# A two-layer mixer network and an attention block on one core: the first block's attention finished in two pairs of heads, the state-space mixer moved in front of it, and w_out's rows reordered

## The chip, the core and the metric

The kernel runs on one core of a Trainium2 chip. Its metric is the device time in microseconds, here the median of three runs. A profiled execution, taken separately, gives the trace; its span goes from the first to the last instruction.

## The reference

Two blocks in a row work on x, 256 tokens by 1024, in float32. The first has two layers, the second one. The change is in the first block, in the mixers of each layer:

```python
xn = rms_norm(h, attn_norm_g[layer])
u_ssm, u_g, v_g, q, k, v = split(xn @ w_in[layer])        # 256, 256, 256, 512, 512, 512 columns
y_ssm  = s5_mixer(u_ssm, ...)        # linear recurrence per 16-channel group, GELU, GLU with w_glu
y_sgu  = spatial_gating(u_g, v_g, ...)   # u * (W_s v + b) over windows of 128
y_diff = diff_attention(q, k, v, ...)    # 4 heads, two soft-maxes each, then rms_norm per head
h = h + concatenate([y_ssm, y_sgu, y_diff]) @ w_out[layer]   # rows 0-255, 256-511, 512-1023
h = h + conv_gated_mlp(rms_norm(h, ffn_norm_g[layer]), ...)
```

The second block (another attention with memory, gates and an output projection) is not touched.

## The kernel before

**Precision and tiling.** A large product is made of three matmuls on parts of the operands: high times high, high times low, low times high. Weights come from HBM as 1 MB pieces (`wraw`) on SyncE's queue, in the order in which `st.add` listed them; ScalarE makes the high part (L152), VectorE the low part (L153), each 128x1024, with five such buffers. Activations are kept transposed, as `xh` and `xl`, in eight blocks of 128 rows by 256 tokens; `mix` holds the mixers' output in that form: blocks 0 and 1 from the state space, 2 and 3 from gating, 4 to 7 from the four heads.

**What sets the order.** The Python code lists the instructions, and a scheduler puts each engine's instructions into one fixed order, by priority and by when its model holds them ready. Priority is the place in the listing, except that the gemms of a layer's mixers stand 3000 places later (`low`), and the weight splits some places later (`SPLIT_...`). Each engine runs its order strictly. The mixers are generators. A plan string says in which order gemms and mixer steps are listed: `k q u A2 S2 v g G* A* S*` for layer 0 means the gemms of k, q and the state-space input u, two steps of the attention, two of the state space, the gemms of v and of the gating inputs, then gating, attention and state space to their ends. Layer 1 has `k u q S6 A2 v g S* G* A* m`, where m is the gemm of the second block's memory values.

**The mixers.** The state space (`ssm_gen`, L885) shuffles its input by 16 small DMAs, transforms it in two halves a=0 and a=1 (L902; VectorE reads each from the bank px), scans along time (L917), forms the states (L920 to L929), and sums in a bank yb the skip taps (`ktap`, L934) and the outputs of the states (`ct`, L941). Then follow GELU (L945), the w_glu product (L951), tanh, add one, the gate product and the split into high and low parts (L962). Gating (`gmlp_gen`, L965) takes its row statistics, then two products in px (L982).
The attention (`diff_gen`, L1090) has eight units, four heads by two query halves q. `scores` makes a score bank, the soft-maxes and their weighted difference; `values`, two units behind, transposes this (bank pt, of which there is one), multiplies by the values, and adds up squares. When all eight are done, one `rsqrt` of 8 columns (nine small VectorE operations, L371 to L381) gives the norm, and for each query half the four heads are scaled, transposed in pt (L1145) and split (L665, L666).

**PSUM.** Four banks `acc` for gemms and for yb, two for scores, one pt, and one px for the small products of the state space and gating.

**w_out** (L1299 to L1306) takes all four `acc` banks, two token halves by two column halves. For each of four pairs of row blocks, in the order `OUT_ORDER`, it issues 24 matmuls, six to a bank: (2, 4, 6, 0) in layer 0, that is gating, heads 0 and 1, heads 2 and 3, state space; (0, 2, 4, 6) in layer 1. The residual sum and the next norm (L1195) follow.

Of the kernel before, what the change touches and what calls it, by code (L numbers as in the profile page):

```python
# [15 lines left out]
AF = mybir.ActivationFunctionType  # L16
# [4 lines left out]
P = 128  # L21
S = 256
# [5 lines left out]
LOW_1 = 3000  # L28
LOW_2 = 29
DMA_STEPS = 3  # L30
PLAN0 = "k q u A2 S2 v g G* A* S*"
PLAN1 = "k u q S6 A2 v g S* G* A* m"
SPLIT_L0 = 200
SPLIT_F0 = 60
# [132 lines left out]
def tile_model(tc, t, out):  # L167
# [26 lines left out]
    def acc():  # L194
        return Bank(nc, pacc.tile([P, 512], F32, name=nm("acc"), tag="acc"))
# [4 lines left out]
    def pst():  # L200
        return Bank(nc, ps.tile([P, 512], F32, name=nm("pt"), tag="t", bufs=PST_BUFS))
# [32 lines left out]


    PLAN = (PLAN0, PLAN1)
    OUT_ORDER = ((2, 4, 6, 0), (0, 2, 4, 6))
    for l in range(LAYERS):
        w = t["w_in"][l]
        if l == 1:  # L240
# [127 lines left out]
    def rsqrt(src, n, scale, dst=None, tag=None):  # L368

        v = sm(n, tag=tag)  # L370
        V.tensor_scalar(v, src, scale, EPS, op0=OP.mult, op1=OP.add)  # L371
        i = sm(n, I32, tag=(tag or "sm") + "i")
        V.tensor_scalar(i, v.bitcast(I32), 1, None, op0=OP.logical_shift_right)
        V.tensor_scalar(i, i, -1.0, float(0x5F3759DF), op0=OP.mult, op1=OP.add)
        y = i.bitcast(F32)
        z = sm(n, tag=tag)
        for it, d in enumerate((8.77e-4, 5.8e-7)):
            V.tensor_tensor(z, y, y, op=OP.mult)
            V.scalar_tensor_tensor(z, z, -0.5 * (1 + d), v, op0=OP.mult, op1=OP.mult)
            o = dst if (it == 1 and dst is not None) else sm(n, tag=tag)  # L380
            V.scalar_tensor_tensor(o, z, 1.5 * (1 + d), y, op0=OP.add, op1=OP.mult)  # L381
            y = o
        return y
# [22 lines left out]
    def tt(o, a, b_, op, eng=None):  # L406
        (eng or V).tensor_tensor(o, a, b_, op=op)  # L407
# [477 lines left out]
    def ssm_gen(l, ut, mix):  # L885
# [36 lines left out]
        for ri in range(2):  # L922
# [4 lines left out]
            p1v, p2v = [x.rearrange("p (j m) -> p j m", j=8)[:, :, :63] for x in (p1, p2)]  # L927
            tt(st_[ri][:, :, 1:], p1v, p2v, OP.subtract if ri else OP.add)
            yield  # L929
        yb = acc()  # L930
        yv = yb.t.rearrange("p (a i m) -> p a i m", a=2, i=4)
        for a in range(2):
            for i in range(4):
# [156 lines left out]
    def diff_gen(l, qts, sc, vv, mix):  # L1090

        ob = [gen(), gen()]
        ss = sm(8)

        def scores(hd, q):
            nk = P * (q + 1)
            bk = pss()
            sv = bk.t.rearrange("p (c k) -> p c k", c=2)[:, :, :nk]
            bk.mm(sv, qts[hd // 2][:, hd % 2, q * P : (q + 1) * P], kz[hd][:, :, :nk])
            bk.mm(sv[:, :, nk - P : nk], identb, maskd.unsqueeze(1).to_broadcast([P, 2, P]), stop=True)  # L1100
            p = gen()
            pv_ = p.rearrange("p (c k) -> p c k", c=2)[:, :, :nk]
            l_ = sm(2)
            softmax_rows(sv, nk, 2, sc[:, q * 8 + hd * 2 : q * 8 + hd * 2 + 2], pv_, l_)
            rl = sm(2)
            V.reciprocal(rl, l_)
            V.tensor_tensor(rl[:, 1:2], rl[:, 1:2], nlam[:, l : l + 1], op=OP.mult)
            V.tensor_scalar(pv_[:, 1, :], pv_[:, 1, :], rl[:, 1:2], None, op0=OP.mult)
            V.scalar_tensor_tensor(pv_[:, 0, :], pv_[:, 0, :], rl[:, 0:1], pv_[:, 1, :], op0=OP.mult, op1=OP.add)
            return p  # L1110

        def values(hd, q, p):
            nk = P * (q + 1)
            bk = pst()
            for kt in range(q + 1):
                T.transpose(bk.t[:, kt * P : (kt + 1) * P], p[:, kt * P : (kt + 1) * P], ident)
            wt_ = gen()
            A.copy(wt_[:, :nk], bk.t[:, :nk])
            po = bk.t[:, S : S + P]
            for kt in range(q + 1):  # L1120
                T.matmul(po, lhsT=wt_[:, kt * P : (kt + 1) * P],
                         rhs=vv[kt][:, hd * P : (hd + 1) * P], start=kt == 0, stop=kt == q)
            A.copy(ob[q][:, hd * P : (hd + 1) * P], po)
            A.activation(p[:, :P], po, AF.Square, accum_out=ss[:, q * 4 + hd : q * 4 + hd + 1])

        units = [(hd, q) for hd in range(4) for q in range(2)]
        ahead = []
        for u in units:
            ahead.append((u, scores(*u)))
            yield  # L1130
            if len(ahead) > 2:
                u, p = ahead.pop(0)
                values(*u, p)
                yield
        for u, p in ahead:
            values(*u, p)
            yield
        rs = rsqrt(ss, 8, 1.0 / P)
        for q in range(2):
            on = ob[q]  # L1140
            ov_ = on.rearrange("p (h e) -> p h e", h=4)
            tt(ov_, ov_, rs[:, q * 4 : q * 4 + 4].unsqueeze(2).to_broadcast([P, 4, P]), OP.mult)
            bk = pst()
            for hd in range(4):
                T.transpose(bk.t[:, hd * P : (hd + 1) * P], on[:, hd * P : (hd + 1) * P], ident)  # L1145
            bv = bk.t.rearrange("p (h s) -> p h s", h=4)
            split_scaled(mix[0][:, 4:8, q * P : (q + 1) * P], mix[1][:, 4:8, q * P : (q + 1) * P], bv, sgl[:, l : l + 1])
            yield


    kmT = const.tile([P, 4, S], F32, name="kmT")
# [670 lines left out]
```

## Time and profile before

| | |
|---|---|
| three runs | 1047.45, 1050.00, 1050.54 us (median 1050.0) |
| profiled execution | 1047.36 us |
| its span | 1045.1 us |
| TensorE (matmul / weight load) | 1001.7 us (96%) / 893.2 us (85%) |
| VectorE, ScalarE, GpSimd | 772.0 (74%), 618.0 (59%), 14.5 us (1%) |
| mean granted TensorE clock | 0.994 |
| layer 0: mixers and w_out | about 40 to 140 us |
| layer 1: mixers and w_out | about 362 to 470 us |

Matmul records overlap, since matmuls are pipelined: one that lasts 0.39 us in its row is followed 0.23 us later by the next. Lengths of stretches are therefore taken from starts.

### The profile page before, as it was taken

Reading aid. Unit: us, or ns where it says so; the run is one execution under the profiler, and the core shown is the slowest. Engines: PE = TensorE matmul, PEld = TensorE weight load, DVE = VectorE, ACT = ScalarE, POOL = GpSimd, SP = SyncE. Lnnn points to the kernel's source line nnn. Section 1 sums busy time; section 2 is a strip of 40 time slices with the busy share of each in tenths; the row PEclk is TensorE's granted clock in tenths of the full one; section 3 lists DMA queues with packets and bytes.
Section 4 is the critical chain, followed back from the end, with each engine's and each line's share of the span. In section 5 each row is a group of like instructions: output and inputs, shape, how many; then the busy total and the mean of one; then the engine's idle time right before and its main releaser. Section 6 shows DMA issues by size and latency. Waiting matters only on the chain.

```text
span 1045.1 us, 18439 instructions
## 1 busy us (share of the span) xinstructions
PE 1001.7 (96%) x7177; PEld 893.2 (85%) x7177; DVE 772.0 (74%) x1561; ACT 618.0 (59%) x1207; POOL 14.5 (1%) x34
## 2 busy tenths in 40 slices
PE   6799899999999999999999999999999999999996
PEld 5677689999998888778999999899787899889995
DVE  6989789887888669758777777776665666446675
ACT  5786567655675577757555555645666555544442
POOL 2000000000000000000000000000000000000000
PEclk9899999999999999999999999999999999999998
DMA  6543153556555544244554655667332535425551
GB/s 193 195 161 129 51 178 125 199 191 208 197 185 168 185 143 162 81 160 157 168 201 163 201 173 190 194 193 239 121 122 81 170 113 182 131 86 195 167 179 40
DMA packets 130494, 166.57 MB, mean 159 GB/s; under 512 B 12050, under 2 KB 103272, under 8 KB 130408
## 3 DMA queue, kind: packets, MB, share of 16 engines
q1 hardware_dynamic: 130376, 165.40, 48.4%
q8 instruction: 56, 0.92, 0.4%
q14 instruction: 30, 0.25, 0.1%
q10 hardware_dynamic: 32, 0.01, 0.0%
HBM read 160.15 MB, written 1.05 MB: 154 GB/s over the span
## 4 chain that ended last, share of the span: by engine, by line
PE 82%; DVE 8%; ACT 6%; issue 2%; DMA 1%; SPq 0%; POOL 0%; ACTq 0%; DVEq 0%; POOLq 0%
PE acc L94 48%; PE ps L94 26%; DVE sgen L407 2%; DVE wlo L153 2%; PE pt L1479 1%; ACT whi L152 1%; ACT sgen L598 1%; ACT gen L1002 1%; DMA wraw<-in_w_in_dram 1%; PE acc L1534 1%; PE acc L1625 1%; DMA wraw<-in_w_mem_kv_dram 1%; PE px L902 0%; DVE sgen L917 0%; PE acc L1536 0%
## 5 line engine op out<-in xcount | busy, mean ns | idle before, releaser
L152 ACT ACTIVATE whi<-wraw 128x1024 fp32r<-128x1024 f32 x294 | 310.0, 1061 | 270.5 <-PE acc L94 145.1
L153 DVE TENSOR_TENSOR wlo<-wraw,whi 128x1024 fp32r<-128x1024 f32 x294 | 358.0, 1222 | 117.1 <-ACT whi L152 115.1
L94 PE MATMUL ps<-xh,whi 128*128 128x256 f32 x736 | 208.9, 285 | 3.2 <-ACT xh L665 3.2
L94 PE MATMUL ps<-xl,whi 128*128 128x256 f32 x736 | 208.5, 283 | 0.2 <-DVE xl L666 0.2
L94 PE MATMUL ps<-xh,wlo 128*128 128x256 f32 x736 | 208.5, 283 | 0.0
L94 PE MATMUL acc<-xh,wlo 128*128 128x256 f32 x544 | 158.1, 291 | 4.3 <-DVE wlo L153 4.3
L94 PE MATMUL acc<-xh,whi 128*128 128x256 f32 x544 | 158.5, 292 | 0.8 <-ACT xh L665 0.7
L94 PE MATMUL acc<-xl,whi 128*128 128x256 f32 x544 | 157.1, 289 | 0.1
L94 PE MATMUL acc<-whi,xh 128*128 128x512 f32 (+1 forms) x416 | 150.6, 365 | 4.7 <-ACT xh L665 3.4
L94 PE MATMUL acc<-wlo,xh 128*128 128x512 f32 (+1 forms) x416 | 151.2, 363 | 1.9 <-DVE wlo L153 1.8
L94 PE MATMUL acc<-whi,xl 128*128 128x512 f32 (+1 forms) x416 | 149.5, 362 | 0.0
L94 PEld LDWEIGHTS ps<-xh,whi 128*128 128x128 f32 x736 | 140.8, 192 | 5.0 <-ACT xh L665 4.1
L94 PEld LDWEIGHTS ps<-xl,whi 128*128 128x128 f32 x736 | 141.1, 192 | 1.5 <-DVE xl L666 0.6
L94 PEld LDWEIGHTS ps<-xh,wlo 128*128 128x128 f32 x736 | 141.1, 192 | 0.0
L94 PEld LDWEIGHTS acc<-xh,wlo 128*128 128x128 f32 x544 | 105.2, 193 | 5.9 <-DVE wlo L153 4.7
L94 PEld LDWEIGHTS acc<-xh,whi 128*128 128x128 f32 x544 | 105.1, 194 | 3.2 <-issue 1.3
L94 PEld LDWEIGHTS acc<-xl,whi 128*128 128x128 f32 x544 | 105.2, 193 | 2.2 <-issue 1.5
L94 PEld LDWEIGHTS acc<-whi,xh 128*128 128x128 f32 x416 | 79.3, 191 | 16.9 <-ACT xh L665 4.8
L94 PEld LDWEIGHTS acc<-wlo,xh 128*128 128x128 f32 x416 | 79.5, 191 | 13.5 <-DVE wlo L153 3.5
L94 PEld LDWEIGHTS acc<-whi,xl 128*128 128x128 f32 x416 | 79.0, 190 | 10.2 <-DVE xl L666 0.3
L94 PE MATMUL acc<-whi,ah 128*128 128x512 f32 x176 | 69.9, 397 | 0.3 <-ACT ah L669 0.3
L94 PE MATMUL acc<-wlo,ah 128*128 128x512 f32 x176 | 69.5, 395 | 0.0
(339 smaller groups left out, 1396.9 us busy)
## 6 DMA issues: line engine op xcount, KB each, us to landing
wraw<-in_w_in_dram SPq DMA_DIRECT2D x58, 1024.0 KB
wraw<-in_w_up_dram SPq DMA_DIRECT2D x44, 1024.0 KB
wraw<-in_w_down_dram SPq DMA_DIRECT2D x22, 1024.0 KB
wraw<-in_w_out_dram SPq DMA_DIRECT2D x12, 1024.0 KB
wraw<-in_w_mem_kv_dram SPq DMA_DIRECT2D x4, 1024.0 KB
gen<-gen SPq DMA_DIRECT2D x48, 64.0 KB
wraw<-in_w_br_b_dram SPq DMA_DIRECT2D x2, 1024.0 KB
wraw<-in_w_br_m_dram SPq DMA_DIRECT2D x2, 1024.0 KB
```

Source lines behind the costliest of these rows:

```text
L94: self.nc.tensor.matmul(out, lhsT=lhsT, rhs=rhs, start=not self.open if start is None else start, stop=stop)
L152: self.nc.scalar.activation(hv, part, AF.Copy)
L153: self.nc.vector.tensor_tensor(lv, part, hv.bitcast(F32), op=OP.subtract)
L407: (eng or V).tensor_tensor(o, a, b_, op=op)
L598: A.copy(pd[ps, hf], bpow[ri][ps, a * 4 : a * 4 + 4])
L1002: A.activation(sq[:, i * 64 : i * 64 + 64], src[:, i * 64 : i * 64 + 64], AF.Square, scale=rstd[:, q : q + 1], accum_out=ss[:, i : i + 1])
L1479: T.transpose(bk.t[:, i * P : (i + 1) * P], p[:, i * P : (i + 1) * P], ident)
L1534: T.matmul(oc, lhsT=pt[:, kt * P : (kt + 1) * P], rhs=vs[0][:, kt, cols], start=kt == 0, stop=False)
L1625: T.matmul(oc, lhsT=pt[:, (i * 2 + kt) * P : (i * 2 + kt + 1) * P], rhs=vb[:, kt, kv * 64 : kv * 64 + 64], start=kt == 0, stop=kt == 1)
```

## The change

Layer 0's plan lists the state space before the attention, and its w_out takes gating, state space, heads 0 and 1, heads 2 and 3. In both layers yb is taken from px in place of `acc`, and the attention normalises, transposes and splits heads 0 and 1 as soon as their four units have their values, and heads 2 and 3 at the end. The sums of squares lie in another order of columns for that.

```diff
-PLAN0 = "k q u A2 S2 v g G* A* S*"
+PLAN0 = "k q u A2 S2 v g G* S* A*"
...
-    OUT_ORDER = ((2, 4, 6, 0), (0, 2, 4, 6))
+    OUT_ORDER = ((2, 0, 4, 6), (0, 2, 4, 6))
...
-        yb = acc()
+        yb = psx()
...
-            A.activation(p[:, :P], po, AF.Square, accum_out=ss[:, q * 4 + hd : q * 4 + hd + 1])
+            A.activation(p[:, :P], po, AF.Square, accum_out=ss[:, hd * 2 + q : hd * 2 + q + 1])
...
+        def finish(hp):
+            rs = rsqrt(ss[:, hp * 4 : hp * 4 + 4], 4, 1.0 / P)
+            bk = pst()
+            bv = bk.t.rearrange("p (h q s) -> p h q s", h=2, q=2)
+            for q in range(2):
+                on = ob[q][:, hp * S : (hp + 1) * S]
+                ov_ = on.rearrange("p (h e) -> p h e", h=2)
+                tt(ov_, ov_, rs.rearrange("p (h q) -> p q h", q=2)[:, q].unsqueeze(2).to_broadcast([P, 2, P]), OP.mult)
+                for h in range(2):
+                    T.transpose(bv[:, h, q], on[:, h * P : (h + 1) * P], ident)
+            k = 4 + hp * 2
+            split_scaled(mix[0][:, k : k + 2, :].rearrange("p h s -> p (h s)"),
+                         mix[1][:, k : k + 2, :].rearrange("p h s -> p (h s)"), bk.t, sgl[:, l : l + 1])
+
+        done = []
+        def take_values():
+            (hd, q), p = ahead.pop(0)
+            values(hd, q, p)
+            done.append(hd)
+            yield
+            if len(done) % 4 == 0:
+                finish(hd // 2)
+                yield
+
         for u in units:
             ahead.append((u, scores(*u)))
             yield
             if len(ahead) > 2:
-                u, p = ahead.pop(0)
-                values(*u, p)
-                yield
-        for u, p in ahead:
-            values(*u, p)
-            yield
-        rs = rsqrt(ss, 8, 1.0 / P)
-        for q in range(2):
-            on = ob[q]
-            ov_ = on.rearrange("p (h e) -> p h e", h=4)
-            tt(ov_, ov_, rs[:, q * 4 : q * 4 + 4].unsqueeze(2).to_broadcast([P, 4, P]), OP.mult)
-            bk = pst()
-            for hd in range(4):
-                T.transpose(bk.t[:, hd * P : (hd + 1) * P], on[:, hd * P : (hd + 1) * P], ident)
-            bv = bk.t.rearrange("p (h s) -> p h s", h=4)
-            split_scaled(mix[0][:, 4:8, q * P : (q + 1) * P], mix[1][:, 4:8, q * P : (q + 1) * P], bv, sgl[:, l : l + 1])
-            yield
+                yield from take_values()
+        while ahead:
+            yield from take_values()
```

## Rows read from the trace of the kernel before

**Rows 1.** The page's first part: engine, busy us (share of the span), instructions.
```profile
PE 1001.7 (96%) x7177; PEld 893.2 (85%) x7177; DVE 772.0 (74%) x1561; ACT 618.0 (59%) x1207; POOL 14.5 (1%) x34
```
**Rows 2.** Windows of both layers' mixers: length, busy per engine, clock, DMA.
```profile
90.00:106.00 16.00, 13.49 (x83) 10.23 (x82) 13.86 (x50) 10.86 (x43) 0.00 (x0) 1.00 0.36 131
106.00:120.00 14.00, 10.51 (x169) 7.31 (x168) 12.69 (x41) 5.53 (x20) 0.00 (x0) 1.00 0.04 9
...
420.00:450.00 30.00, 30.00 (x164) 23.33 (x162) 21.03 (x60) 21.30 (x68) 2.14 (x4) 1.00 0.20 70
```
**Rows 3.** Chain of waits, end of w_out in layer 0: start, us, what.
```profile
119.76 1.20 PE acc L94 x4
...
123.82 15.38 PE acc L94 x68
```
**Rows 4.** Timeline, the state space behind its second transform, VectorE and ScalarE.
```profile
106.27 0.69 DVE L407 TENSOR_TENSOR sgen<-px,tab 128x512 f32<-128x512 f32 x1 [0.72 <-PE px L902]
106.88 0.68 DVE L670 TENSOR_TENSOR xl<-sgen,xh 128x512 fp32r<-128x512 f32 x1
...
115.31 0.17 DVE L373 TENSOR_SCALAR sm<-sm 128x8 int32<-128x8 int32 x1
...
115.43 0.68 DVE L407 TENSOR_TENSOR sgen<-sgen,sgen 128x504 f32<-128x504 f32 x1
...
119.75 1.28 ACT L945 ACT_TABLE_LOAD   x1
...
121.04 0.60 ACT L945 ACTIVATE sgen<-acc 128x512 f32<-128x512 f32 x1
...
123.85 0.84 ACT L955 ACTIVATE sgen<-px,bgh 128x256 f32<-128x256 f32 x2 [1.64 <-PE px L951]
...
125.53 0.63 ACT L957 ACTIVATE sgen<-sgen 128x512 f32<-128x512 f32 x1
...
126.81 1.30 DVE L407 TENSOR_TENSOR sgen<-sgen,sgen 128x512 f32<-128x512 f32 x1
...
128.15 0.64 ACT L665 ACTIVATE xh<-sgen 128x512 fp32r<-128x512 f32 x1 [1.04 <-DVE sgen L407]
```
**Rows 5.** Timeline of TensorE: skip taps, second transform, first and last w_out matmul.
```profile
83.57 1.37 PE L94 MATMUL acc<-ut,ktap 128*128 128x256 f32 x8
...
104.04 1.07 PE L902 MATMUL px<-sgen,bt 128*128 128x64 f32 x8
...
106.54 0.50 PE L94 MATMUL acc<-whi,xh 128*128 128x512 f32 x1
...
139.53 0.39 PE L94 MATMUL acc<-whi,xl 128*128 128x512 f32 x1
```
**Rows 6.** Timeline of ScalarE: gating's statistics, last exponential, last sum of squares.
```profile
91.21 1.06 ACT L152 ACTIVATE whi<-wraw 128x1024 fp32r<-128x1024 f32 x1 [1.00 <-PE acc L94]
92.17 0.40 ACT L971 ACTIVATE sgen<-vt 128x256 f32<-128x256 f32 x1
...
106.91 0.57 ACT L1087 ACTIVATE gen<-ps,sm,sc 128x256 f32<-128x256 f32 x1
...
114.38 0.20 ACT L1124 ACTIVATION_READ_ACCUMULATOR gen<-pt 128x1 f32 x1
```
**Rows 7.** Timeline of layer 1: output products, w_glu product, table load for exponentials.
```profile
413.14 2.00 PE L94 MATMUL acc<-sgen,ct 128*32 128x64 f32 x128
...
418.75 2.00 PE L951 MATMUL px<-sgen,wglu 128*128 128x256 f32 x8 [0.63 <-ACT sgen L945]
...
423.37 1.28 ACT L1087 ACT_TABLE_LOAD   x1
```
**Rows 8.** Timeline of VectorE in layer 1: first step of the attention's reciprocal root.
```profile
447.55 0.17 DVE L371 TENSOR_SCALAR sm<-sm 128x8 f32<-128x8 f32 x1 [3.37 <-ACT gen L1124]
```
**Rows 9.** Timeline of TensorE, and its window, after a long idle time.
```profile
44.52 0.58 PE L94 MATMUL acc<-xh,wlo 128*128 128x256 f32 x1 [4.01 <-DVE wlo L153]
...
44.50:49.60 5.10, 5.08 (x24) 5.08 (x25) 5.10 (x11) 4.11 (x17) 0.99 (x2) 0.50 0.00 2
```

## The prediction

> **What bounds the kernel now.** I read the busy line first: TensorE holds 1001.7 of 1045.1 us [rows 1], so a change can win only out of the 43 us in which it stands still, unless it alters the work, and it doesn't: the matmuls and transposes are the same in number. Then the windows around the first layer's mixers [rows 2]: from 90 to 106 us TensorE lacks 2.5 us, from 106 to 120 3.5, and after that nothing up to 140. Those 6.0 us are all there is to win in layer 0. VectorE is the fuller engine there (12.7 of 14 us between 106 and 120). In layer 1's mixers, 420 to 450 us, TensorE is full (30.00 of 30), because the memory-value product lies under them.
>
> The chain of waits and the timeline show the order. w_out has 96 matmuls, four groups of 24, one group for two row blocks. Group 2 (gating) starts at 106.54 [rows 5], 18 of its 24 run before the attention is done; group 4 waits for the attention to 119.76; from 123.82 on 68 matmuls take 15.38 us without a break, 0.226 each [rows 3], and the last starts at 139.53 [rows 5]. The state-space rows (hi part from 128.15 on [rows 4]) are last in line and hold nobody up.
>
> **What the change does to that.** Matmuls into one bank keep program order: each w_out bank takes its rows as OUT_ORDER has them. With (2, 0, 4, 6) the state-space group is second, so the attention groups wait behind it in all four banks. After the change the end of w_out is set by R, the time at which the state-space rows are ready: three groups, 72 x 0.226 = 16.3 us, follow R. Today's end is 139.53 + 0.23 = 139.8, so the change breaks even at R = 139.8 - 16.3 = 123.5. Today's R is 128.15 + 0.64 = 128.8. The question is whether the state-space chain gains 5.3 us.
>
> **Its chain, step by step.**
> - *Input transform of half a=1.* It needs the one px bank, which the gating mixer uses from its second product until shortly before 104; it starts at 104.04 [rows 5], VectorE at 106.27 [rows 4]. Gating stays ahead of the state space in the plan, so this start stays, except for what gating itself gains (below).
> - *VectorE.* From 106.27 to 116.1 the chain occupies 9.8 us; nine other operations lie in it, the first the gating low part at 106.88, the last a reciprocal-root step at 115.31 [rows 4], by their start times 2.0 us together (0.6 gating, 1.4 attention). Its own share is 7.8. In front of the attention only gating's 0.6 must come first: 114.7. Where a chain operation waits for the one before, attention steps will still slip in. Bounds: none and all of the attention's 1.4 plus the first pair's finish, about 2.1 (nine small steps at 0.1, which is what the one at 115.31 holds the next operation up, two half-width products at 0.35, a low part at 0.6). I take 0.5, nearer to none because most junctions have a second chain operation ready: 115.2.
> - *Output products.* 128 short matmuls, 2.00 us in layer 1 where nothing breaks them [rows 7]. In layer 0 they are broken at present by the attention's transposes and end at 119.7. Now 117.2.
> - *GELU.* Table load 1.28 plus 0.60 [rows 4]: 119.1.
> - *w_glu product* 2.00 [rows 7]: 121.1. *Tanh pair* 0.84: 121.95. *Add one* 0.63: 122.6. *Gate product* 1.30: 123.9. *High part* 0.64: 124.55 [rows 4]. At present two weight splits push themselves between the last steps; the banks' waiting time lets these be made earlier, since group 2 frees its weight buffers near 112. If they still stand there, R is 1.5 later: 0.84 between the tanh's end at 124.69 and the add, 0.65 between its end at 126.16 and the product [rows 4].
>
> So R = 124.55 without any lead. **The lead:** the skip-tap matmuls (ktap) fill an accumulator now up to 84.94, on a full TensorE; the last eight of the sixteen take 1.37 us [rows 5], all of them so 2.7. In px they can run only after the a=1 transform is read, near 108; there they lie under VectorE's stretch. What is queued behind them at 82, the last gating product, ends up to 2.7 us sooner. Gating's own statistics stand on ScalarE at 92.17 right behind a weight split that waited 1.00 us for TensorE [rows 6]. Bounds 0 and 2.7; I take 0.7, under the 1.00 of that wait, which is the nearest row: the rest of gating's chain waits for VectorE, which doesn't become freer. R = 123.85, and the end 140.2: 0.4 later than now.
>
> **The rest of the edits.**
> - *yb in px.* It frees an accumulator: the six group-2 matmuls that now wait for its release after the GELU (121.64) run before 113, in an idle stretch; already in the sum. px is held through the GELU; nobody else asks for it then, because gating comes before in layer 0 and after the w_glu product in layer 1.
> - *Finishing in pairs.* Per layer nine more small VectorE steps (0.17 each alone, 447.55 [rows 8], about 0.2 apart); the normalising products are four of half width for two of full width. In layer 1 VectorE has gaps (21.0 of 30 us) and TensorE is full, so nothing. New is a wait: the first pair's finish takes the one pt bank between the fourth and fifth value units; queued behind it on TensorE and ScalarE are those four units' transposes and copies. That is 1.6 to 3 us of root steps, 0.7 product, 0.6 transposes, 0.7 and 0.75 splits: about 5 us. The attention's last sum of squares is read at 114.58 [rows 6] and its first rows come at 119.7; five later is some 123 to 125 with the second finish. Group 6 needs them at R + 48 x 0.226 = 134.7, so 10 us of cover. Without that cover this would cost its whole 5.
> - *The swapped plan* issues no DMA in another place, as the shuffle copies belong to the steps before; the order of w_out's loads changes, and that costs nothing: the chain waits for none of them between 119.76 and 139 [rows 3]. The last exponential is over at 107.5 [rows 6] and the GELU comes after it, so no second table switch in layer 0.
> - *Layer 1* keeps its order and is full on TensorE [rows 2]: 0, with bounds of -0.7 and +0.7 for gaps at its seams. Behind it all other code is the same; a shifted list of instructions may win or lose 1 us there.
>
> A rule on table switches would say more. ScalarE pays 1.28 us for the load here and the GELU starts 1.29 us after the load does [rows 4]; in layer 1 the switch back is 1.28 too, and no idle time stands in front of it [rows 7]. The Trainium skill (ScalarE: Activation LUTs, What ACT_TABLE_LOAD costs) counts a drain with every switch, 2.66 us in all. By that R would be 1.4 us later and the end 141.6. The trace shows no such drain in front of a load, so I stay with 1.28.
>
> **Sum.** +0.4 in layer 0, about 0 elsewhere: 1047.36 of the profiled execution becomes 1047.8. Its three timed runs reached 1047.45 to 1050.54, mean 1049.3; on that scale 1049.5, half a microsecond under the median shown. 0.3% (3.15 us) is about what can be told from no change.
>
> **Rivals.**
> 1. *Faster: the chain leads and gaps fill.* If the a=1 transform slips in front of gating's use of px, or gating gains the whole 2.7, R falls to 119 to 122. TensorE then sets the end: of the 6.0 us idle some 2.5 remain: -3.5, so 1046. For it: gating's statistics start only at 92.17 [rows 6], and its products need px after that. Against: px was as free before and was not taken early. With small gains elsewhere it reaches -5. Chance 0.3.
> 2. *Slower: the swap doesn't speed the chain.* If attention steps and weight splits keep their places, R stays between 126.7 and 128.8, while w_out now stands behind it: 128.8 + 16.3 = 145.1, +5.3, so 1054.5. It decides from R = 126.65 on (+3.15). For it: VectorE is 91% full there, and the far bounds together (1.4 + 2.1 - 0.5 on VectorE, 1.5 by weight splits) add 4.5 to R. Against: priority alone should move most of them. Chance 0.17.
> 3. *Slower: the clock.* Between group 2 and R TensorE has only scraps. At 44.5 us, after TensorE had stood still for 4.01, the clock granted was 0.50 for 5.1 us, its lower level of 1.2 GHz [rows 9]: some 2.5 us lost. With +0.4 and a late R: +3.5, 1053. Against: from 106 to 120 TensorE is 75% busy and keeps 1.00 [rows 2], and the skip taps and values now fall into that time. The Trainium skill (TensorE: Matmul & The Clock Gate, HAM oscillation) warns of idle gaps between bursts; the trace's stretch from 44.5 us agrees. Chance 0.08.
>
> **How the numbers follow.** No measurable change 0.45, own range 1047 to 1052; rival 1 0.3; rivals 2 and 3 0.25. From these: faster 0.3, same 0.45, slower 0.25. The range reaches into both: 1044.5 (rival 1 with -5) to 1054.5 (rival 2).
>
> **What would show it.** Right: group 2 complete near 112; then no w_out matmul until R near 124; after it one unbroken run of 72 and the residual's transposes near 140; the skip taps after 107. Each step's mark: VectorE's last state near 115.2, the GELU's end near 119, the first attention pair's split near 110, its second by 125. Wrong: w_out matmuls of the attention before the state-space rows (then order in the bank isn't what I think), R under 120 or over 126.6, a granted clock under 1.00 between 112 and 126, or an exponential with its own table load behind the GELU.

## The result, and the profile after

The changed kernel is slower. Its median over five runs is 1056.62 us (1053.95 to 1058.19), that of the kernel before on the same chip 1049.35; the ratio is 1.0067 with an interval of [1.0046, 1.0088], 7.0 us. The forecast was 1049.5 with a range up to 1054.5. The profiled execution of the changed kernel took 1053.95 us, its span is 1052.2.

The first part of its page (engine, busy us, share of the span, instructions) answers to [rows 1]: the matmuls are the same 7177, VectorE has 22 instructions more, ScalarE two.

```profile
PE 1007.0 (96%) x7177; PEld 894.4 (85%) x7177; DVE 774.7 (74%) x1583; ACT 620.0 (59%) x1209; POOL 14.3 (1%) x34
```

Two executions don't begin their mixers at the same moment, so I count from a mark M, the start of the ten transform matmuls of half a=0, which no edit touches. The two rows of before, from TensorE's timeline (start, us, engine, line, what), are M and the first transposes of the residual behind w_out's last matmul:

```profile
87.70 1.23 PE L902 MATMUL px<-sgen,bt 128*128 128x64 f32 x10
...
139.77 0.60 PE L1208 MATMUL pt<-ident,xraw 128*128 128x128 f32 x4
```

The same timeline of the changed kernel, with the steps of layer 0 that matter:

```profile
86.28 1.22 PE L902 MATMUL px<-sgen,bt 128*128 128x64 f32 x10
...
101.91 1.90 PE L902 MATMUL px<-sgen,bt 128*128 128x64 f32 x16
...
112.84 1.88 PE L94 MATMUL px<-sgen,ct 128*32 128x64 f32 x120
114.92 0.77 PE L1138 MATMUL pt<-ident,gen 128*128 128x128 f32 x4 [0.19 <-DVE gen L407]
...
117.87 3.01 PE L951 MATMUL px<-sgen,wglu 128*128 128x256 f32 x8 [1.95 <-ACT sgen L945]
120.67 0.42 PE L1116 MATMUL pt<-ident,gen 128*128 128x128 f32 x1
...
124.45 0.80 PE L94 MATMUL acc<-whi,xh 128*128 128x512 f32 x1 [0.38 <-ACT xh L665]
125.04 0.63 PE L94 MATMUL acc<-wlo,xh 128*128 128x512 f32 x1
...
137.40 0.68 PE L1138 MATMUL pt<-ident,gen 128*128 128x128 f32 x4 [0.19 <-DVE gen L407]
...
145.65 0.60 PE L1220 MATMUL pt<-ident,xraw 128*128 128x128 f32 x4
```

From M to the residual it was 139.77 - 87.70 = 52.07 us; it is 145.65 - 86.28 = 59.37. That is +7.3, about the whole loss: the spans differ by 7.1 us, since M came 1.4 us earlier (in both executions the clock was at half rate ahead of M, for 6.8 us before and 3.4 here) and the stretch to layer 1's w_out took 1.2 us more. The state-space rows are ready at 124.45, 38.17 behind M. But the attention's fifth unit is transposed only at 120.67 (L1116) and the second pair at 137.40; before, the last sum of squares of the last unit was read at 114.58 [rows 6].

ScalarE's timeline of the changed kernel shows what came between:

```profile
102.27 0.28 ACT L1124 ACTIVATE gen<-pt 128x128 f32<-128x128 f32 x1
...
115.36 0.46 ACT L1087 ACTIVATE gen<-ps,sm,sc 128x128 f32<-128x128 f32 x1 [3.45 <-DVE tab L407]
...
115.93 1.28 ACT L945 ACT_TABLE_LOAD   x1
117.22 0.60 ACT L945 ACTIVATE sgen<-px 128x512 f32<-128x512 f32 x1
...
118.41 1.28 ACT L1087 ACT_TABLE_LOAD   x1
119.71 0.46 ACT L1087 ACTIVATE gen<-ps,sm,sc 128x128 f32<-128x128 f32 x1
...
123.22 0.57 ACT L1087 ACTIVATE gen<-ps,sm,sc 128x256 f32<-128x256 f32 x1
...
138.12 0.69 ACT L665 ACTIVATE xh<-pt,sgl 128x512 fp32r<-128x512 f32 x1 [3.00 <-PE pt L1138]
```

Exponentials (L1087) stand ahead of the GELU at 117.22 and behind it, with a table load of their own at 118.41. The last exponential of before was at 106.91 [rows 6].

VectorE's timeline of the changed kernel, the first step and the last of each pair's reciprocal root:

```profile
102.68 0.17 DVE L371 TENSOR_SCALAR sm<-sm 128x4 f32<-128x4 f32 x1 [0.30 <-ACT gen L1124]
...
114.04 0.15 DVE L381 SCALAR_TENSOR_TENSOR sm<-sm,sm 128x4 f32<-128x4 f32 x1
114.11 0.42 DVE L1080 TENSOR_REDUCE sm<-ps 128x2 f32<-128x256 f32 x1
...
133.01 0.17 DVE L371 TENSOR_SCALAR sm<-sm 128x4 f32<-128x4 f32 x1 [4.38 <-ACT gen L1124]
...
136.63 0.16 DVE L381 SCALAR_TENSOR_TENSOR sm<-sm,sm 128x4 f32<-128x4 f32 x1
```

Nine steps that take 1.8 us when nothing comes between (the second pair's in e2 below) took 11.5 for the first pair, since the state space goes first on VectorE. On TensorE the finish's transposes (114.92) stand ahead of the fifth unit's (120.67) in the one bank pt, so units 5 to 8 wait for the finish. The row maxima of the seventh unit (L1080) come right behind the last step, at 114.11.

Windows of the changed kernel (length, busy us of TensorE, its weight loads, VectorE, ScalarE, GpSimd, then the granted clock, the DMA engines' busy share and GB/s):

```profile
90.00:106.00 16.00, 11.18 (x58) 7.71 (x58) 13.58 (x53) 8.61 (x32) 0.00 (x0) 1.00 0.28 96
106.00:120.00 14.00, 11.45 (x171) 9.05 (x172) 10.38 (x31) 6.27 (x9) 0.00 (x0) 0.95 0.23 77
...
116.00:118.00 2.00, 0.13 (x1) 0.13 (x2) 0.00 (x0) 1.99 (x3) 0.00 (x0) 1.00 1.04 362
118.00:120.00 2.00, 2.00 (x7) 1.66 (x8) 0.75 (x1) 1.97 (x3) 0.00 (x0) 0.67 0.09 32
120.00:122.00 2.00, 1.13 (x5) 0.43 (x3) 1.50 (x6) 1.34 (x6) 0.00 (x0) 0.50 0.02 5
...
128.00:130.00 2.00, 2.00 (x10) 1.53 (x9) 0.56 (x3) 1.02 (x3) 0.00 (x0) 0.77 0.00 0
```

Against [rows 2] TensorE is busy 0.9 us more between 106 and 120, where the skip taps now lie, and 2.3 less between 90 and 106. After 116 to 118, busy for 0.13 of 2 us, its clock was at the lower level, 1.2 GHz, from about 118.7 to 128.9: w_glu's product took 3.01 us where 2.00 was reckoned, and w_out's first products follow each other 0.43 us apart and not 0.23.

### The profile page after: what moved, and what is told of

Its sections match the earlier page's. It is cut to its first block, busy times and chain, and to the rows that moved or that the text cites. A ratio compares the mean times of both kernels' runs of the same rounds, so it can differ in the third digit from the quotient of the medians.

```text
span 1052.2 us, 18463 instructions
## 1 busy us (share of the span) xinstructions
PE 1007.0 (96%) x7177; PEld 894.4 (85%) x7177; DVE 774.7 (74%) x1583; ACT 620.0 (59%) x1209; POOL 14.3 (1%) x34
## 4 chain that ended last, share of the span: by engine, by line
PE 84%; DVE 7%; ACT 5%; issue 2%; DMA 2%; SPq 1%; POOL 0%; ACTq 0%; POOLq 0%; DVEq 0%
PE acc L94 48%; PE ps L94 27%; DVE wlo L153 2%; DVE sgen L407 2%; PE pt L1491 1%; ACT whi L152 1%; DMA wraw<-in_w_in_dram 1%; PE pt L1121 1%; ACT gen L1002 1%; PE acc L1546 1%; PE px L902 1%; PE px L94 1%; PE acc L1637 1%; ACT sgen L598 1%; DMA gen<-in_lambda_k_dram 1%
## 5 line engine op out<-in xcount | busy, mean ns | idle before, releaser
L153 DVE TENSOR_TENSOR wlo<-wraw,whi 128x1024 fp32r<-128x1024 f32 x294 | 358.2, 1222 | 118.2 <-ACT whi L152 116.1
```

The lines of the kernel that those rows point to most:

```text
L153: self.nc.vector.tensor_tensor(lv, part, hv.bitcast(F32), op=OP.subtract)
```

## The experiments

Twelve kernels ran. Columns of times: ratio to the kernel before in the same job, median, and from the one profiled execution of each the distance from M to w_out's end in layer 0; in that stretch, how long TensorE stood idle and how long its clock was at half rate (granted clock 0.50, 1.2 GHz); the distance from there to w_out's end in layer 1; and the part of it that is layer 1's own (its gemms, mixers and w_out). The other part, ahead of it, is layer 0's MLP, which no edit touches.

| kernel | ratio [95% interval] | median us | M to end, layer 0 | idle in it | half rate in it | layer 1 | its own part |
|---|---|---|---|---|---|---|---|
| before | 1 | 1049.35 | 52.07 | 6.0 | 0 | 330.53 | 116.7 |
| changed | 1.0067 [1.0046, 1.0088] | 1056.62 | 59.37 | 9.4 | 10.2 | 331.71 | 117.0 |
| e2 pairs only | 1.0038 [1.0022, 1.0054] | 1053.03 | 53.50 | 6.2 | 0 | 333.64 | 117.5 |
| e4 bank only | 0.9978 [0.9965, 0.9990] | 1047.03 | 52.40 | 5.8 | 3.4 | 329.34 | 116.0 |
| e5 swap only | 1.0035 [1.0019, 1.0051] | 1053.33 | 56.87 | 8.9 | 3.4 | 331.25 | 116.7 |
| e6 changed, no pairs | 1.0013 [1.0000, 1.0026] | 1050.56 | 55.17 | 7.9 | 3.4 | 329.52 | 116.2 |
| e7 changed, no swap | 1.0005 [0.9995, 1.0015] | 1050.04 | 52.01 | 5.5 | 0 | 332.16 | 117.0 |
| e1 changed, finishes late | 1.0035 [1.0019, 1.0050] | 1052.28 | 56.68 | 7.3 | 10.2 | 330.46 | 115.9 |
| e8 first finish after six units | 1.0039 [1.0027, 1.0051] | 1053.40 | 58.74 | 7.8 | 13.7 | 330.02 | 116.7 |
| e9 e1 with the old rows | 1.0029 [1.0017, 1.0041] | 1052.00 | 58.95 | 9.2 | 10.2 | 329.48 | 116.1 |
| e3 own small tiles | 1.0061 [1.0041, 1.0082] | 1055.41 | 59.31 | 10.9 | 6.8 | 330.58 | 115.8 |
| e11 finishes late in layer 1 | 1.0058 [1.0043, 1.0072] | 1056.19 | 59.28 | 10.3 | 6.8 | 330.89 | 115.9 |
| e10 extra products | 1.0101 [1.0085, 1.0116] | 1061.02 | 63.02 | 9.7 | 6.8 | 330.92 | 116.6 |
| e12 bank in layer 1 only | 0.9980 [0.9969, 0.9991] | 1047.89 | 54.54 | 5.7 | 6.8 | 329.78 | 115.9 |

**The clock in these figures.** TensorE is busy for 46.1 us between M and w_out's end before and for 49.9 in the changed kernel, though the matmuls are nearly the same (358 and 354 records). So +7.3 is 3.4 us more of idle time and 3.9 of longer work, since for 10.2 us it ran at half rate. Windows of that stretch (columns as above), before, changed, e1, e6:

```profile
87.70:139.77 52.07, 46.06 (x358) 36.16 (x357) 42.54 (x131) 29.55 (x86) 0.00 (x0) 1.00 0.40 128
86.28:145.65 59.37, 49.93 (x354) 38.27 (x353) 44.41 (x144) 31.54 (x87) 0.00 (x0) 0.91 0.35 113
87.67:144.35 56.68, 49.35 (x355) 38.34 (x354) 43.43 (x144) 30.44 (x86) 0.00 (x0) 0.91 0.38 122
86.80:141.97 55.17, 47.23 (x355) 37.19 (x354) 42.51 (x133) 30.29 (x86) 0.00 (x0) 0.97 0.37 119
```

The timed runs say about the same. Each has its mean granted clock on record, and with it the time at half rate: 18 us on average over the 81 runs of the kernel before, 28 in the changed kernel, 28 in e1, 25 to 27 in e3, e10 and e11, 23 in e5 and e8, 22 in e9, 20 in e6 and e7, 16 to 17 in e2, e4 and e12. Between runs of one kernel, 1 us more at half rate goes with 0.30 us more of time (a fit over these 81 runs and the 107 of the other kernels, each kernel on each chip about its own mean; it takes up 81% of the scatter). By this estimate about 3 of the changed kernel's 7.0 us, and about 3 of e1's 3.7, go with the lower clock. Differences of one profile by a microsecond or two, and those between kernels with unlike clocks, are to be read with that in mind.

The theory after the comparison of traces was that the first pair's finish holds up units 5 to 8 (finish theory). Its rivals: the new order of work does it whatever the finish does (order theory), and TensorE's clock does it.

**e1: both finishes after the eighth unit**

```diff
             done.append(hd)
             yield
-            if len(done) % 4 == 0:
-                finish(hd // 2)
-                yield
...
         while ahead:
             yield from take_values()
+        for hp in range(2):
+            finish(hp)
+            yield
```

> The changed kernel with one thing undone: both pairs of heads are finished after the eighth value unit, none in the middle. Holding theory (the first pair's finish, listed between the fourth and fifth value units, keeps the later units waiting, because the small tiles and the bank pt are handed out in listing order while its root steps wait behind the state space on VectorE): all exponentials come before the GELU, no extra table loads (1 at the GELU, none behind), the state-space rows are ready 2 to 3 us sooner, TensorE's clock stays at 1.00 between 112 and 130, and the time falls by 5 to 8 us against the changed kernel, to 1048 to 1052 (0.998 to 1.002 of before). Order theory (the loss is w_out standing behind the state-space rows, whatever the attention does): nothing of this, 1054 to 1058.

About half of the loss is gone, 1052.28 against the 1048 to 1052 that the holding theory allowed. The exponentials are ahead of the GELU, and one table load stands there. The clock stayed at 1.00 from 112 to 130 as expected, but in this profile it stood at half rate from 93.9 to 104.1 us, the a=1 transform came 18.84 behind M in place of 15.63, and the state-space rows were 1.0 us later and not earlier. TensorE's idle time is 7.3 us against 9.4, only 1.3 above before. So what is left of the loss goes with the clock for the most part, and not with the order of work alone.

**e2: the pairs alone, in the kernel before** (plan, row order and yb's bank as before)

```diff
+        def finish(hp):
...
-        rs = rsqrt(ss, 8, 1.0 / P)
...
+            if len(done) % 4 == 0:
+                finish(hd // 2)
+                yield
```

> The kernel before with only the finishing in two pairs (old plan, old order of w_out, yb in an accumulator). Holding theory: in front of the state space the first pair's root steps have priority on VectorE, so they take 2 to 3 us and not 11; the last exponentials move by about 5 us but stay before the GELU; w_out gets heads 0 and 1 early, near 110. Time 1046 to 1051, no clock loss. If instead the finish in the middle is bad in any plan: 1053 or more. Order theory: nothing is lost without the new order, 1047 to 1051.

The pairs cost 4.0 us with the attention first, too: the answer "bad in any plan", and the holding theory missed. The first pair's root steps took 6.2 us (103.31 to 109.53) where 2 to 3 were expected. In this profile layer 0 gives 1.4 of the cost and the stretch to layer 1's end 3.1, but only 0.8 of that lies in layer 1's own part; the rest lies in layer 0's MLP, where the clock was at half rate for 3.4 us from 147.0 on.

**e3: the changed kernel, the finish's root steps in small tiles of their own**

```diff
-    SM_BUFS = {"sme": 2, "sth": 2, "smi": 3, "smg": 6, "smgi": 2}
+    SM_BUFS = {"sme": 2, "sth": 2, "smi": 3, "smg": 6, "smgi": 2, "smf": 8, "smfi": 2}
...
-            rs = rsqrt(ss[:, hp * 4 : hp * 4 + 4], 4, 1.0 / P)
+            rs = rsqrt(ss[:, hp * 4 : hp * 4 + 4], 4, 1.0 / P, tag="smf")
```

> The changed kernel, the pair's root steps with small tiles of their own (8 and 2 buffers), so that the soft-max of the units behind it isn't in line behind them; the bank pt is still held. Holding theory, by small tiles alone: exponentials of unit 7 at about 103 in place of 115, and the one of unit 8 with them, most of the loss comes back: 1048 to 1052. By tiles and pt together: unit 7 early, unit 8 still behind the GELU with one or two extra table loads, a part comes back: 1051 to 1055. If neither matters: as the changed kernel, 1054 to 1058.

No gain that can be told. Unit 7's exponentials moved ahead of the GELU, unit 8's stayed behind it: the pattern of the second answer without its gain. The small tiles held unit 7, but they alone don't make the loss; the bank pt stays a candidate. A second bank for the finish would show it alone, but all eight are taken, so it wasn't tried.

**e4: yb in px alone, in the kernel before**

```diff
-        yb = acc()
+        yb = psx()
```

> The kernel before with only yb in px instead of an accumulator. Rival theory (px, of which there is one, held through skip taps, output products and GELU, is what costs): 1053 or more. Holding and order theories: the skip taps move from 82 into idle time near 108 and the fourth w_out bank starts earlier, 1046 to 1050, the gating part of w_out 0.7 us or so sooner.

The one edit that pays, by 2.3 us; the interval ends under 1. TensorE is busy 13.49 of the 14 us from 106 to 120, against 10.51 before [rows 2], and 2.2 us less from 90 to 106, so in layer 0 the idle time is only moved (5.8 us against 6.0). In all ten kernels with the bank in layer 0 TensorE now stands still for 2.97 us from 4.05 behind M, where it was busy before.

**e5: the swap alone, in the kernel before**

```diff
-PLAN0 = "k q u A2 S2 v g G* A* S*"
+PLAN0 = "k q u A2 S2 v g G* S* A*"
...
-    OUT_ORDER = ((2, 4, 6, 0), (0, 2, 4, 6))
+    OUT_ORDER = ((2, 0, 4, 6), (0, 2, 4, 6))
```

> The kernel before with the state-space mixer put ahead of the attention and w_out's rows in the new order, and nothing else: no pairs, the output products still in an accumulator. The finish theory (the pairs hold up units 7 and 8, and the new order only exposes it): all exponentials of the first layer stand ahead of the GELU, two table loads fewer than in the changed kernel, w_out ends within 2 us of before, 1048 to 1051 us. The order theory (putting the state space first leaves the attention's last steps between w_out's products whatever the finish does): 1052 us or more, as with the finishes put late (1052.3). The clock theory: half rate between 106 and 130 in either case, and then 1053 or more.

It costs 3.7 us by itself, and all exponentials are ahead of the GELU, so the order theory holds for this part: 2.9 us more of idle time. The clock theory's signs came too (half rate from 115.0 to 118.4, over 1053), and a part of the 3.7 goes with it. TensorE's timeline of this kernel: the state-space rows come at 125.53, 37.71 behind M, and the attention's two finishes now lie between w_out's products.

```profile
125.53 0.50 PE L94 MATMUL acc<-whi,xh 128*128 128x512 f32 x1 [1.73 <-ACT xh L665]
...
131.65 0.63 PE L1145 MATMUL pt<-ident,gen 128*128 128x128 f32 x4
...
134.08 0.60 PE L1145 MATMUL pt<-ident,gen 128*128 128x128 f32 x4
```

**e7: the changed kernel without the swap**, that is the diff of e5 backwards

> The changed kernel with the old plan and the old row order, so pairs and the output products off the accumulators. If the parts add up: pairs alone 1.0038 and the bank alone 0.9978 give 1.0016, 1051 us, and then the swap is worth the remaining 5 us of the changed kernel. If the pairs' cost comes from the waits for VectorE behind the state space, and those are there in either order: 1050 to 1052 with w_out's end 1 to 2 us later than with the bank alone. If the loss is the bank's together with the pairs (both now ask for banks that other steps use): 1055 as in the changed kernel.

1050.04: bank and pairs add up within the scatter (1051 by adding), and layer 0 is as short as before. The swap on top makes 1.0067 of 1.0005, 6.5 us, against 3.7 by itself (e5). So swap and pairs seem to make each other worse by some 2.8 us: with the attention first the pairs cost 2.8 (e4 to e7), behind the state space twice that (e6, below). The intervals of the four kernels leave this as 0 to 6 us, and the changed kernel has, with e1, the lowest clock.

**e8: the first finish after the sixth unit's values**

```diff
-            if len(done) % 4 == 0:
-                finish(hd // 2)
+            if len(done) in (6, 8):
+                finish(len(done) // 2 - 3)
```

> The changed kernel with the first pair's finish written after the sixth unit's values instead of the fourth, so behind the eighth unit's scores; everything else as changed. The finish theory (the steps of units 7 and 8 are handed their tiles behind the finish's): both units' exponentials come before the GELU, one table load fewer in the stage, the first pair's transposes still ahead of the second's, 1051 to 1053 us, no worse than with both finishes last (1052.3). A rival, that any finish ahead of the last values costs what it cost in the change: 1055 or more. The clock theory alone does not tell it from the finish theory.

1.0039 against the changed kernel's 1.0067 (the intervals overlap from 1.0046 to 1.0051), and no worse than e1: the place of the first finish is worth about 3 us. Both units' exponentials came before the GELU, with one table load, as the finish theory has it. What is left does not go away with it; this profile has 13.7 us at half rate and 1.8 us more of idle time than before.

**e9: e1 with w_out's rows in the old order**

```diff
-    OUT_ORDER = ((2, 0, 4, 6), (0, 2, 4, 6))
+    OUT_ORDER = ((2, 4, 6, 0), (0, 2, 4, 6))
```

> The changed kernel with both finishes after the eighth unit, as in the run with the finishes put late, and besides w_out's rows in the order of before (state-space rows last). If what is left of the loss there (1052.3) is that the state-space rows stand early in w_out: 1049 to 1051. If the attention's rows are now the late ones (their last transposes at 130.6 us there, the state-space rows at about 123), then the 24 products of the state-space rows no longer fill the wait and come behind it, 24 x 0.226 us = 5.4 us at most: 1054 to 1057.

Neither: 1052.0 against 1052.28 in e1. Which group of rows stands second makes no difference in time that can be told here, while state space and attention both end late. In the two profiles e9 has 1.9 us more of idle time; by the timed runs' clocks e1 stood longer at half rate.

**e10: nine products more, to keep TensorE busy at 116 us**

```diff
         A.activation(yg, yb.t, AF.Gelu_apprx_tanh)
+        if l == 0:
+            wb = psx()
+            s3 = st_[1].rearrange("p j m -> p (j m)")
+            for _ in range(9):
+                T.matmul(wb.t[:, :S], lhsT=ident, rhs=s3[:, :S], start=True, stop=True)
```

> The changed kernel with nine products of the identity by the last state tile added in the first layer, behind the output products and ahead of w_glu's, into a bank that nobody reads: about 9 x 0.24 us = 2.1 us of TensorE work in the gap from 115.9 to 117.9 us. Nothing else is changed. The clock theory: the stretch from 118.5 to 128.5 keeps its full rate, w_glu's product takes 2.0 us instead of 3.0 and the products behind it 0.23 instead of 0.43 us apart, and the kernel gains 1.5 to 3 us: 1053.5 to 1055. If the half rate is only a companion of the loss (what waits there is the attention, not TensorE): full rate, and the time stays within 1 us of 1056.6. If the gap is not what lowers the clock: half rate and the same time.

Inconclusive, and my mistake: there is one bank px, so the products waited for the GELU to read yb and then stood ahead of w_glu's product. In the trace they are 18 matmuls and not nine, and took 5.84 us and not 2.1. TensorE's timeline of this kernel:

```profile
118.75 5.84 PE L950 MATMUL px<-sgen,ident 128*128 128x256 f32 x18 [1.96 <-ACT sgen L945]
...
124.65 1.99 PE L956 MATMUL px<-sgen,wglu 128*128 128x256 f32 x8
```

The state-space rows came 4.8 us later behind M than in the changed kernel and w_out's end 3.65 later, so w_out's end still follows those rows.

**e11: both finishes late in layer 1 only**

```diff
-            if len(done) % 4 == 0:
+            if l == 0 and len(done) % 4 == 0:
                 finish(hd // 2)
...
+        if l == 1:
+            for hp in range(2):
+                finish(hp)
+                yield
```

> The changed kernel with both finishes after the eighth unit in the second layer only; the first layer as changed. From one w_out's end to the next the changed kernel took 331.71 us in its profile, the one with the finishes late in both layers 330.46 and the one before 330.53. If the pairs cost something in the second layer too, as these rows say: 1.2 us less than the change, 1055.4, and that distance back at 330.5. If that distance only scatters from run to run: 1056.6 within 0.7.

The times don't decide: 1056.19 agrees with the second answer, the ratio of 1.0058 (1055.4 beside the changed kernel's own before) with the first. Layer 1's own part does: 115.9 us here, in e1 and (116.1) in e9, which all have the bank and late finishes there; 117.0, 116.6 and 117.0 in the changed kernel, e10 and e7, which have the bank and the early finish. So the early finish costs about 1 us there. In e3, where it has small tiles of its own, the part took 115.8 us, as without it.

**e12: yb in px in layer 1 only, in the kernel before**

```diff
-        yb = acc()
+        yb = psx() if l else acc()
```

> The kernel before with the output products off the accumulators in the second layer only. With the bank in both layers the second layer took 1.2 us less from w_out's end to w_out's end (329.34 against 330.53 in the profiles) and w_glu's product there came 4.0 us earlier, while the first layer saw a half-rate stretch from 95 to 98.5 us that the kernel before does not have. If the gain is the second layer's and the first gives none: 1047.6, with full rate from 90 to 106. If the first layer's share counts (1047.0 with both): 1048 or more. If the whole of it is scatter: 1049.

0.9980, the same as with the bank in both layers: the gain is layer 1's as far as the times tell, though one profile's stretch there shows only 0.75 us of the 2.1 (1.2 in e4), nearly all in layer 1's own part (115.9 against 116.7). About 1 us more goes with the clock, by the estimate above: 16 us at half rate against 20 in the kernel before of the same job. This kernel and e4 beat both the kernel before and the changed one; between them there is nothing to tell.

**e6: the changed kernel without the pairs** (one finish for all heads after the eighth unit, as before)

```diff
-        yb = acc()
+        yb = psx()
...
-PLAN0 = "k q u A2 S2 v g G* A* S*"
+PLAN0 = "k q u A2 S2 v g G* S* A*"
...
-    OUT_ORDER = ((2, 4, 6, 0), (0, 2, 4, 6))
+    OUT_ORDER = ((2, 0, 4, 6), (0, 2, 4, 6))
```

> The changed kernel with the attention heads finished as before, after all eight units, by token halves and not by pairs of heads; the new plan, row order and bank stay. If the parts add up (swap alone 1.0035, bank alone 0.9978): 1.0013, 1050.9 us; what the kernel with both finishes late has above that (1.0035) is then the pairs themselves, in the second layer most of all, where w_out's end to w_out's end took 333.6 us with pairs alone against 330.5 before. If the swap leaves the bank nothing to give: 1.0035 as with the finishes late, 1053.

1.0013, what adding gives. So the changed kernel's +7.0 us is, with the pairs taken last: bank -2.3, swap +3.7, pairs 1.0067 - 1.0013 = 0.0054 or +5.7. Of these 5.7 the pairs cost 2.3 when both finishes come late (e1 over e6), and the early place of the first the other 3.4. The 2.3 is hardly the finish's own: e1's profile has less idle time than e6's (7.3 us against 7.9), and its timed runs stood 7 us longer at half rate, some 2.1 us by the estimate. The 3.4 is at an equal clock (28 us in both): 2.1 us of idle time in layer 0 and about 1 in layer 1.

## Why the prediction was wrong

**What held.** In e6, where the attention finishes as before, the state-space chain is the one that the prediction worked out, and TensorE's timeline shows its result:

```profile
86.80 1.23 PE L902 MATMUL px<-sgen,bt 128*128 128x64 f32 x10
...
117.32 1.99 PE L951 MATMUL px<-sgen,wglu 128*128 128x256 f32 x8 [0.86 <-ACT sgen L945]
...
122.78 0.50 PE L94 MATMUL acc<-whi,xh 128*128 128x512 f32 x1
```

Predicted was R = 123.85 on before's clock, 36.15 behind M; it is 122.78 - 86.80 = 35.98. In the changed kernel, too, the steps came as said up to the output products: the a=1 transform at 101.91, 15.63 behind M, where 16.34 less a lead of 0.7 was forecast. That a table load has no drain in front of it held in its new place: at 118.41 it begins 0.01 us behind the end of the instruction ahead of it.

**What failed, by steps.**

1. *"About 5 us" of wait for pt, with "10 us of cover" for the attention's rows.* This is the step that broke. The forecast gave the state space the front place on VectorE for its own chain, but did not carry through that the finish's nine root steps then stand behind that same chain: 11.5 us and not 1.6 to 3. With pt next in line for it, units 5 to 8 waited for it. The second pair's transposes were forecast by 125, 37.3 behind M; they came 51.1 behind it. Moving only that finish behind unit 6 brought 0.28% (e8), putting it late 0.32% (e1), taking the pairs out 0.54% (e6). And even without pairs (e6) the last transposes came 43.2 behind M, 10 later than before (33.1): the forecast's 37.3 for them was kept in no version of the swap. That the bank pt is what holds units 5 to 8 is read from TensorE's order and left over by e3; no run frees it alone.

2. *"The last exponential is over at 107.5 and the GELU comes after it, so no second table switch."* 107.5 was read from an execution in which the attention goes first. In the changed kernel units 7 and 8 get their maxima at 114.11 and 120.37, so the GELU stands between exponentials, and a second load of 1.28 us with it. Together with w_glu's product at half clock (3.01 for 2.00), R came at 38.17 behind M, 2.0 later than forecast.

3. *"72 x 0.226 = 16.3 us follow R."* The product count was right, the stretch was not: it took 145.65 - 124.45 = 21.2 us in the changed kernel and 141.97 - 122.78 = 19.2 in e6, where pairs play no part. Between the 72 products lie the attention's transposes and value products, which the forecast had ahead of R: 17 in pt in the changed kernel, 8 in e6. And eight of the products run at half clock, 8 x 0.2 = 1.6 us. The rest, 3.3 us in the changed kernel and 1.3 in e6, is the work in pt, in part at half clock too: TensorE hardly waits any more there (busy for 21.01 of 21.20 us, and for all 19.19 in e6). So the break-even at R = 123.5 was too late by about 3 us; that is why the swap loses even where R comes out as forecast.

   The reason is one of cover. Before, TensorE had the attention's 48 products to run while the state-space tail went from engine to engine: from 123.82 on it never stops [rows 3]. After the swap the attention's products stand behind the state space's 24 in every bank, and its rows are later as well, so nothing of w_out is left to run beneath the state-space tail: TensorE stands still for 9.2 us between M and R in the changed kernel and for 7.9 in e6, where it was 6.0 in all before, and the attention's own work comes behind R.

4. *Layer 1: 0.* This came out, by two terms that cancel. Layer 1's own part took 117.0 us in the changed kernel and 116.7 before. The bank brought 0.5 to 0.8 there (e4, e6, e12), at the edge of the -0.7 that I allowed: the w_glu product came at 414.72 in e4's profile, 418.75 before [rows 7]. The early finish cost 0.8 (e2) to 1 us (e11). "TensorE is full, so nothing" was wrong for both.

5. *Small slips.* The mean of the three runs and +0.4 make 1049.7 and not 1049.5; the first pair's finish adds up to 2.2 and not 2.1. Neither changes the answer.

Two of the signs of being wrong that the prediction named came: a granted clock under 1.00 between 112 and 126, and an exponential with its own table load behind the GELU. The first pair's split, expected near 110, that is 22.3 behind M, began at 117.72, 31.4 behind M.

**The rivals.** Rival 2 gave the right side, for another reason: the chain did speed up. Its 1054.5 was close to the measured time by chance. Rival 3 (clock, 0.08) was a larger part than its chance says, and its price of 2.5 us was about right: by the rows 1.6 us behind R and 1.0 at w_glu, by TensorE's busy time 3.9 of the 7.3 in this profile, by the timed runs about 3 of 7.0. It isn't the whole cause: e11 has the same order of TensorE's work in layer 0 as the changed kernel, but its clock fell later, at about 124, and w_glu's product took 1.99. Windows of e11, columns as above:

```profile
118.00:120.00 2.00, 1.11 (x5) 1.01 (x6) 0.56 (x1) 1.97 (x4) 0.00 (x0) 1.00 0.54 182
...
124.00:126.00 2.00, 1.34 (x3) 1.14 (x4) 1.97 (x16) 2.00 (x5) 0.00 (x0) 0.50 0.36 72
```

Its w_out ended 59.28 behind M, the changed kernel's 59.37; it stood at half rate for 6.8 us in place of 10.2 and was idle for 10.3 in place of 9.4. What the loss would be with no half-rate stretch at all wasn't shown; e10 was to show it. By the estimate some 4 us would be left, the early finish's 3.4 first of all.

## What to carry to other kernels

When two chains share a saturated engine, moving one in front moves the other's steps back; work out both ends, and count what work the third engine still has beneath the tail of the chain that it then waits for. A step listed early can hold up everything that uses its single-buffered bank behind it, however late its own inputs come: give it its place by when its inputs are ready (e8, e1). Set the idle time and the granted clock of every profile beside its time before an edit gets the credit or the blame. Durations and gaps read from the old order ("it is over by then") must be derived again for the new one, on each engine.

## What the runs showed of the hardware

Nearly the same idle time may or may not lower TensorE's clock. In all ten kernels with the bank in layer 0 TensorE stands still for 2.97 us from 4.05 behind M. In four of the ten profiles the clock then fell, 6 to 7 us behind M, for 3.4 us (e4, e9) or 10.2 us (e1, e8), and the a=1 transform came 17.0 or 18.8 behind M; in six it did not fall there, and the transform came 15.6 to 15.7 behind M. Windows of e1, then of e6 (columns as above):

```profile
91.67:93.67 2.00, 0.05 (x1) 0.00 (x0) 1.72 (x4) 1.98 (x6) 0.00 (x0) 1.00 1.03 389
94.00:104.00 10.00, 8.49 (x19) 5.25 (x20) 6.82 (x39) 5.00 (x21) 0.00 (x0) 0.50 0.18 56
```

```profile
90.80:92.80 2.00, 0.05 (x1) 0.00 (x0) 1.72 (x4) 1.98 (x6) 0.00 (x0) 1.00 1.07 368
94.00:104.00 10.00, 8.15 (x45) 5.79 (x45) 8.99 (x37) 6.23 (x27) 0.00 (x0) 1.00 0.01 4
```

What a stretch at half rate costs on a full TensorE shows behind layer 1's w_out, where all fourteen kernels run the same code to the end of the span: 574.7 to 575.0 us in six profiles, 575.9 to 576.2 in six with one more such stretch of 3.4 us, 577.5 in two with two more. That is 1.2 to 1.3 us each.

Layer 0 of e12 has the same order of TensorE's instructions as the kernel before. Windows of both (columns as above), the kernel before first:

```profile
112.00:114.00 2.00, 1.28 (x7) 0.67 (x5) 2.00 (x5) 0.89 (x2) 0.00 (x0) 1.00 0.00 0
114.00:116.00 2.00, 0.33 (x9) 0.16 (x8) 2.00 (x7) 0.53 (x3) 0.00 (x0) 1.00 0.00 0
...
118.00:120.00 2.00, 1.55 (x41) 1.25 (x42) 1.07 (x3) 0.94 (x2) 0.00 (x0) 1.00 0.04 8
```

```profile
112.00:114.00 2.00, 0.71 (x4) 0.52 (x4) 2.00 (x7) 1.08 (x5) 0.00 (x0) 1.00 0.00 0
114.00:116.00 2.00, 0.85 (x46) 0.69 (x49) 2.00 (x16) 0.00 (x0) 0.00 (x0) 1.00 0.00 0
...
118.00:120.00 2.00, 2.00 (x41) 1.50 (x39) 0.61 (x2) 0.69 (x1) 0.00 (x0) 0.50 0.03 8
```

From 112 to 116 us TensorE was busy for 1.61 us in the one and 1.56 in the other. In e12 the clock stayed at half to about 123 us, and w_out ended 54.54 behind M, not 52.07: one such stretch (6.8 us) was 2.5 us here, as much as any one edit gains. The Trainium skill (TensorE: Matmul & The Clock Gate, HAM oscillation) warns of idle gaps between bursts; here the lower level did follow a gap, but the same order of work also passed such a gap at full rate.
